# Second block: bias tables from one window per head, kept masks, norms beside the next values, residuals a tile ahead and slabs issued by ScalarE

## The chip, the cores and the metric

One of the eight cores of a Trainium2 chip runs the whole program. Its engines are TensorE (PE: matrix products and transposes into PSUM), VectorE (DVE), ScalarE (ACT), GpSimd (POOL) and SyncE (SP), which issues DMA transfers. Each engine works through its own list of instructions in order and waits on semaphores. The metric is device microseconds (us) of one execution; the profiler's span goes from the first to the last instruction of one profiled execution.

## The reference, cut to what matters

Two blocks run one after the other on a sequence of 1024 tokens, 1024 wide. The first block (dilated attention and a state-space mixer) is not touched. The second block has two layers; the first also carries a context of 256 tokens to a new value, the second does not.

```python
def hybrid_layer(x, xc, c_act, cc_act, w_mod, b_mod, w_in, conv_w, conv_b,
                 ret_decay, na_rpb, w_out, ln_g, ln_b, need_ctx):
    shift, scale, gate = jnp.split(c_act @ w_mod + b_mod, 3, axis=-1)
    h = x * (1 + scale[:, None]) + shift[:, None]
    rk, rv, nk, nv, rq, rg, nq, ng, ch, cb, ccg, cz = split_cols(h @ w_in, PROJ_SPLITS)
    ...
    y_conv = short_conv_branch(ch, cb, ccg, cz, conv_w, conv_b)
    y_ret, yc_ret = retention_branch(...)       # 6 heads, both directions, chunks of 128,
                                                # head_norm(o) * silu(g)
    y_na, yc_na = neighbourhood_branch(...)     # 6 heads, window of 8 x 16 on a 16 x 64 grid, plus the context
    y = jnp.concatenate([y_conv, y_ret, y_na], axis=-1) @ w_out
    x_new = layer_norm(DEEPNORM_ALPHA * x + gate[:, None] * y, ln_g, ln_b)
```

In the neighbourhood branch the score of a query and a key is their product times 1/8, plus a learned bias `rpb[head, dr, dc]` that depends on the difference of rows and columns alone; keys outside the window are left out, and one softmax goes over the 128 keys of the window and the 256 of the context.

## The kernel before, in words

`hybrid()` runs once for each layer. Every product with a weight is done as three products of rounded parts: `w_split` (L154, L155) has ACT round a raw weight tile `wr` to `wh` and DVE take the rest `wl`; the activations lie in SBUF as `aTh` and `aTl` (context: `cTh`, `cTl`). `project` runs 24 matmuls of 128x512 (L168) for each half of the tokens and 24 of 128x256 for the context, into the PSUM tag `mm` of two buffers.

Stages of a layer: the first half of the convolution; three pairs of retention heads (`ret_pair`); three pairs of neighbourhood heads (`na_project`, `na_core`), the second half of the convolution beside the last; `out_ln`, the output projection, residual and layer norm. The branches write their outputs, already gated, to `yd` in DRAM.

Work beside the projections stands in a list `bg` of small functions. While the matmuls of a projection are written, `tick` takes the next function from the list every eight matmuls, at the rate that `pace` sets; `drain` runs what is left. A scheduler then orders the instructions of each engine, so that the written order is a guide and not the order itself.

Retention: `raw` copies a projected group (ACT, tile `raw`), and `values`, `keys` and `queries` work on groups of 4, 4 and 2 chunks of 128 tokens. `queries` has five steps: f1 turns the group (transposes `T` on PE, L1515) and rotates it to `rq` with DVE and POOL; f2 turns it back (`qT`, `qw`); f3 makes the scores `S` (L1640) and `PD`; f4 makes the outputs from `PD` and the running states `St` (L1604, L1655, L1658), copies them (`oe`, ACT L1661), transposes them (`O` on PE, L1664) and makes the head norm: square (`sqr`, ACT), sum (`hv`, DVE), rstd (`hv`, POOL L1672, L1673), scaled output `cen` (DVE L1675); f5 transposes `cen` (L1684), multiplies by the gate `sgl` and stores to `yd`. The list `turns` sets in which order the steps of the three groups are taken; the last one is (2, 4), or (1, 4) in the layer without a context output, and `drain` ends a pair before the next pair's values.

Neighbourhood attention: a unit is one of 2 x 4 blocks of 128 queries (`rt`, `m`) for two heads. `s1` makes the scores against the context and the local keys (`S`, L1786) and DVE joins scores and table (`nsb`, L1766, with a running minimum `nmn`); ACT takes the exponent (`nsb`, L1769); `s2` transposes the weights (`T`, L1799, L1800; copies `nPT`, `nPX`), `s3` multiplies with the values `nV`. `nV` is made by `vturn` (L1730), the keys and queries `nk`, `nkz`, `nqq` by `split` (L1480).

A table `tab` holds bias and mask for 128 queries x 3 column places x 384 keys. `tables(rt)` (L1743 to L1753) is called for rt = 0 ahead of a pair's units and for rt = 1 at its third step. It loads the mask (one buffer) and, for each of the two heads, three slices of the padded bias by overlapping rows, and has DVE make 8 x bias + mask in place. All these loads are issued by SP, in its list among weight, gate and output transfers.

`out_ln`: `fetch` (L1947, L1948) loads slabs of `yd` for 256 tokens, `put` (L1951, L1952) rounds them into `aTh` and `aTl`, and the old activations' place is used again. Then for each tile of 128 tokens: load x into a slab's room (L2001, SP), 2 x 24 matmuls, gate product `ys` (DVE L2007), x and sum (L2008), mean (POOL L2014), square (ACT L2016), the norm with the next layer's scale and shift (L2019, L2020), the transposes into `aT` for the next layer (`to_aT`, L215 to L221), and the layer's own output (L2022, L2024), stored to x (L2025). The norm of a tile is written one tile later, as `pend`.

## Time and profile before

| | us |
|---|---|
| median of 3 runs (lowest, highest) | 3215.74 (3212.7, 3221.98) |
| the profiled execution's own time | 3217.48 |
| its span | 3215.5 |
| PE busy in the span | 3103.7 |
| mean granted PE clock | 0.988 of full speed |
| second block | about 1745 to 3215.5 |
| layer 0: retention, neighbourhood, projection | 1831 to 2095, to 2402, to 2550 |
| layer 1: retention, neighbourhood, projection | 2601 to 2846, to 3118, to 3215.5 |

All times in rows are microseconds from the span's start unless marked ns. A row of the timeline gives start, duration, engine, line, operation, written and read tile, the number of like instructions, and in brackets how long the engine stood idle before it and what let it go. A row of the list of waits is a sum over all waits of that kind.

### The profile page before, as it was taken

The numbers are of one execution on the slowest core, as the hardware profiler recorded it, in microseconds if no ns is written. First come the engines' busy times: TensorE is split into PE (matmuls) and PEld (weight loads), VectorE is DVE, ScalarE is ACT, GpSimd is POOL, SyncE is SP. The second block draws the span as 40 slices with busy tenths as digits, with TensorE's granted clock in tenths as the row PEclk, the third lists the DMA queues.
The fourth block names the chain that finished last, engine by engine and source line by source line (L and its number), as shares of the span: only waits on it lengthen the run. The fifth ranks groups of instructions, "written<-read, shape, count | busy, mean of one in ns | idle before, by whom it ended". The sixth has DMA issues, their size and how long they took to land. (4 is left out here: it accounts for less than half of the span.)

```text
span 3215.5 us, 47884 instructions
## 1 busy us (share of the span) xinstructions
PE 3103.7 (97%) x18100; PEld 2549.1 (79%) x18100; DVE 1898.8 (59%) x4099; ACT 1194.1 (37%) x2494; POOL 592.2 (18%) x769
## 2 busy tenths in 40 slices
PE   8999999999999999999999999999999999899998
PEld 6777878777877888787878888878877888778777
DVE  4676686677666658555544544454557854445455
ACT  4222555554555545322432122244352212134351
POOL 0364121112111101111002033300002212210001
PEclk9999999999999999999999999999999999999999
DMA  5465233233233235564442211142234321132232
GB/s 198 149 198 169 65 97 88 80 107 96 80 97 97 74 120 172 178 177 132 150 131 82 69 47 56 42 121 78 62 106 144 101 68 53 47 106 84 76 110 99
DMA packets 338907, 338.02 MB, mean 105 GB/s; under 512 B 29209, under 2 KB 278772, under 8 KB 338676
## 3 DMA queue, kind: packets, MB, share of 16 engines
q1 hardware_dynamic: 338676, 334.97, 34.1%
q8 instruction: 142, 2.33, 0.3%
q14 instruction: 89, 0.73, 0.1%
HBM read 262.22 MB, written 72.67 MB: 104 GB/s over the span
## 5 line engine op out<-in xcount | busy, mean ns | idle before, releaser
L168 PE MATMUL mm<-aTh,wh 128*128 128x512 f32 x2304 | 920.7, 400 | 18.2 <-DVE nk L1480 2.8
L168 PE MATMUL mm<-aTl,wh 128*128 128x512 f32 x2304 | 917.4, 398 | 0.4 <-DVE aTl L221 0.2
L168 PE MATMUL mm<-aTh,wl 128*128 128x512 f32 x2304 | 916.1, 398 | 0.7 <-DVE wl L155 0.7
L168 PEld LDWEIGHTS mm<-aTh,wh 128*128 128x128 f32 x2304 | 437.5, 190 | 110.2 <-issue 5.4
L168 PEld LDWEIGHTS mm<-aTh,wl 128*128 128x128 f32 x2304 | 436.8, 190 | 88.5 <-issue 3.4
L168 PEld LDWEIGHTS mm<-aTl,wh 128*128 128x128 f32 x2304 | 437.7, 190 | 85.3 <-issue 2.9
L155 DVE TENSOR_TENSOR wl<-wr,wh 128x1024 fp32r<-128x1024 f32 x158 | 196.8, 1245 | 191.4 <-ACT wh L154 190.8
L154 ACT ACTIVATE wh<-wr 128x1024 fp32r<-128x1024 f32 x158 | 166.9, 1057 | 329.6 <-PE mm L168 268.3
L475 ACT ACTIVATE sb<-sb,st 128x128 f32<-128x128 f32 (+1 forms) x384 | 170.1, 444 | 259.1 <-DVE st L473 257.3
L168 PE MATMUL mm<-wo,aTh 128*128 128x512 f32 x768 | 241.8, 396 | 7.1 <-DVE ys L2007 3.8
L1205 DVE SCALAR_TENSOR_TENSOR ma<-mw,cact,ma 128x256 f32<-128x256 f32 x336 | 182.4, 547 | 18.1 <-DMA mw<-in_w_mod 12.0
L168 PEld LDWEIGHTS mm<-wo,aTh 128*128 128x128 f32 x768 | 143.9, 190 | 38.1 <-DVE ys L2007 3.9
L473 DVE CUSTOM_DVE_ANT_0 sb<-S,bt 128x128 f32<-128x128 f32 (+1 forms) x384 | 125.2, 345 | 46.3 <-PE T L486 30.2
L168 PE MATMUL mm<-wo,aTl 128*128 128x512 f32 x384 | 151.4, 394 | 0.9 <-DVE aTl L1952 0.9
L427 POOL CAST qk<-kz 64x512 fp32r<-64x512 f32 x64 | 64.6, 1009 | 360.3 <-ACT kz L421 342.6
L1769 ACT ACTIVATE nsb<-nsb,nmn 128x640 f32<-128x640 f32 (+1 forms) x108 | 85.6, 793 | 118.8 <-DVE nmn L1766 106.3
L486 PE MATMUL T<-ident,sb 128*128 128x128 f32 x560 | 104.6, 283 | 12.0 <-DVE mr L1216 4.5
L168 PE MATMUL mm<-vh,aTl 128*128 128x512 f32 x288 | 114.5, 398 | 0.0
L168 PE MATMUL mm<-vh,aTh 128*128 128x512 f32 x288 | 113.8, 395 | 0.0
L168 PE MATMUL mm<-vl,aTh 128*128 128x512 f32 x288 | 113.6, 394 | 0.0
L168 PE MATMUL mm<-cTh,wl 128*128 128x256 f32 x352 | 101.7, 289 | 0.6 <-DVE wl L155 0.6
L168 PE MATMUL mm<-cTl,wh 128*128 128x256 f32 x352 | 101.9, 289 | 0.0
(448 smaller groups left out, 5701.4 us busy)
## 6 DMA issues: line engine op xcount, KB each, us to landing
wr<-in_attn_w_in SPq DMA_DIRECT2D x80, 512.0 KB
wr<-in_w_in SPq DMA_DIRECT2D x64, 512.0 KB
mw<-in_w_mod SPq DMA_DIRECT2D x48, 512.0 KB
tab<-in_c_rpb SPq DMA_DIRECT2D x72, 192.0 KB
vd<-vo SPq DMA_DIRECT2D x48, 256.0 KB
Wb<-wgd SPq DMA_DIRECT2D x96, 128.0 KB
x<-x SPq DMA_DIRECT2D x24, 512.0 KB
x<-in_x SPq DMA_DIRECT2D x16, 512.0 KB
```

The costliest lines, as they stand in the source:

```text
L154: nc.scalar.activation(h, raw, AF.Copy)
L155: nc.vector.tensor_tensor(l, raw, h.bitcast(F32), op=ALU.subtract)
L168: nc.tensor.matmul(out, s_, m_, start=first and i == 0, stop=last and i == len(todo) - 1)
L427: nc.gpsimd.tensor_copy(at(t[o], g, hf), at(h_[r], g, hf))
L473: nc.vector.tensor_tensor_reduce(out=sb[:, :N], in0=sp[:, a * 256:a * 256 + N], in1=b, scale=1.0, scalar=3e38, op0=ALU.add, op1=ALU.min, a ...
L475: nc.scalar.activation(sb[:, :N], sb[:, :N], AF.Exp, bias=mc, scale=-1.0, accum_out=st[:, 1, g, a, n:n + 1])
L486: nc.tensor.transpose(t[:, c:c + 128], Ps[a][:, b * 128:b * 128 + 128], self.ident)
L1205: V.scalar_tensor_tensor(a, L[h][:, k], c, a, op0=ALU.mult, op1=ALU.add)
L1769: ACT.activation(sb[:, :n], sb[:, :n], AF.Exp, bias=mc, scale=-1.0, accum_out=den)
```

## The change

The diff touches `na_masks`, `ret_pair`, `tables`, the calls around them, `fetch` and `out_ln`; the first block is as before.

- Tables: the order of the three column places is turned round, so that the three slices of a head's bias lie in one window of 400 columns (`win`, one load of 128x400) and are read from there by an overlapping view. The two masks of a layer are loaded once, in two buffers. `tables` no longer loads for itself: `fetch(p, rt)` is called right after the previous table is made, one table ahead; `tab` has one buffer for each head instead of two. The second table of a pair is made at the units' fifth step, not the third, and the first one after the values' turns.
- Norms: the last step f5 of a pair's last group is put into `tail` and run four places into the next pair's values, with three empty steps ahead of it. `turns` takes the steps in a slightly changed order.
- The tiles `raw`, `rr`, `k`, `rq` lie in a pool of their own (`early`).
- `out_ln`: x of the next tile is asked for one tile ahead, of the first before the loop; both gate products of a tile are written ahead of its two residual sums.
- Slabs: `fetch` of `yd` is issued by ACT, not SP.

```diff
-        for y, m in enumerate((0, 1, 3)):
+        for y, m in enumerate((3, 1, 0)):
...
+                early = rs.enter_context(tc.tile_pool(name=self.uid("re"), bufs=1, reuse_waits="tile"))
...
+                    if tail:
+                        self.bg.extend([idle, idle, idle, tail.pop()])
+                        self.rate = 1.0
                     raw(values, True)
...
-                    turns = ((0, 0), (0, 1), (1, 0), (0, 2), (0, 3), (1, 1), (2, 0), (0, 4), (1, 2), (1, 3), (2, 1),
-                             (1, 4), (2, 2), (2, 3), (2, 4))
-                    self.bg.extend(late[g][k] for g, k in turns if g < len(late))
+                    turns = ((0, 0), (0, 1), (0, 2), (1, 0), (0, 3), (1, 1), (2, 0), (1, 2), (0, 4), (1, 3), (2, 1),
+                             (2, 2), (1, 4), (2, 3), (2, 4))
+                    turns = [t for t in turns if t[0] < len(late)]
+                    self.bg.extend(late[g][k] for g, k in turns[:-1])
+                    tail.append(late[-1][4])
...
-                self.pace(9 if need_ctx else 6)
+                self.bg.extend([idle, idle, idle, tail.pop()])
+                self.pace(11 if need_ctx else 8)
...
+                masks = [wp.tile([128, 3, 384], F32, name=self.uid("mask"), tag=f"mask{rt}") for rt in range(2)]
+
+                def fetch(p, rt):
+                    TB[p, rt] = []
+                    for a in range(2):
+                        t = wp.tile([128, 400], F32, tag=f"win{a}", name=self.uid("win"))
+                        dr = (0 if rt == 0 else 4) - 8 * rt + 7
+                        off = rpb.offset + (l * 6 + 2 * p + a) * 896 + (6 + dr) * 32 - 1 - 239
+                        src = bass.AP(tensor=rpb.tensor, offset=off, ap=[[32, 8], [1, 16], [1, 400]])
+                        nc.sync.dma_start(t, src)
+                        TB[p, rt].append(t)
+                for rt in range(2):
+                    nc.sync.dma_start(masks[rt], A["c_namask"][:, rt * 3:rt * 3 + 3])
+                    if not rt:
+                        fetch(0, 0)
...
                     def tables(rt):
-                        def f():
-                            mask = wp.tile([128, 3, 384], F32, name=self.uid("mask"), tag="mask")
-                            nc.sync.dma_start(mask, A["c_namask"][:, rt * 3:rt * 3 + 3])
-                            for a in range(2):
-                                t = wp.tile([128, 3, 384], F32, tag=f"tab{a}", name=self.uid("tab"), bufs=2)
-                                for y in range(3):
...
-                                    nc.sync.dma_start(t[:, y], src)
-                                V.scalar_tensor_tensor(t, t, 8.0, mask, op0=ALU.mult, op1=ALU.add)
+                        for a, t in enumerate(TB.pop((p, rt))):
+                            o = wp.tile([128, 3, 384], F32, tag=f"tab{a}", name=self.uid("tab"))
+                            win = bass.AP(tensor=t.tensor, offset=t.offset, ap=[list(t.ap[0]), [8, 3], [1, 384]])
+                            V.scalar_tensor_tensor(o, win, 8.0, masks[rt], op0=ALU.mult, op1=ALU.add)
+                            L["tab", rt, a] = o
+                        if rt == 0:
+                            fetch(p, 1)
+                        elif p < 2:
+                            fetch(p + 1, 0)
...
-                    out = [tables(0), vturn(0), vturn(1), cturn, vturn(2), vturn(3)]
+                    out = [vturn(0), vturn(1), cturn, vturn(2), vturn(3), lambda: tables(0)]
...
-                            if i == 2:
-                                tables(1)()
+                            if i == 4:
+                                tables(1)
...
             def fetch(y, t):
-                nc.sync.dma_start(y[:, 0], yv[:, 0, t:t + 256])
-                nc.sync.dma_start(y[:, 2:8], yv[:, 2:8, t:t + 256])
+                ACT.dma_start(y[:, 0], yv[:, 0, t:t + 256])
+                ACT.dma_start(y[:, 2:8], yv[:, 2:8, t:t + 256])
...
+        xh = fetch()
         for ctx, i in tiles:
...
-            nc.sync.dma_start(x, src[i * 128:(i + 1) * 128, :])
+            if n < len(tiles):
+                xh = fetch()
...
                 V.tensor_tensor(hs[:, c], ps, B["gate"][:, c], op=ALU.mult)
+            for nh in range(2):
+                c = slice(nh * 512, nh * 512 + 512)
                 V.scalar_tensor_tensor(hs[:, c], x[:, c], alpha, hs[:, c], op0=ALU.mult, op1=ALU.add,
```

The order of the instructions moves with it. PE at the end of layer 1's second retention pair, before (`O`, `oe`, `cen` are the norm of the pair's last group, `raw` the next pair's values, `mm` the next values' products):

```order
L1658 MATMUL S_24766<-qw_4328_24723,St_24517 64x128
L1684 MATMUL T_24729<-ident,cen_24700 128x128 x4
L1658 MATMUL S_24766<-qw_4329_24726,St_24518 64x128
L1664 MATMUL O_24785<-ident,oe_24783 128x128 x4
L1684 MATMUL T_24800<-ident,cen_24796 128x128 x4
L1515 MATMUL T_24852<-ident,raw_24841 128x128 x4
L1515 MATMUL T_24888<-ident,raw_24877 128x128 x4
L168 MATMUL mm_25103<-aTh,wh_24915 128x512
L168 MATMUL mm_25103<-aTl,wh_24915 128x512
L168 MATMUL mm_25103<-aTh,wl_24916 128x512
```

After, the same place, up to the first products (the line numbers are those of the changed kernel, six higher here):

```order
L1664 MATMUL S_24753<-qw_4338_24710,St_24504 64x128
L1664 MATMUL S_24753<-qw_4339_24713,St_24505 64x128
L1521 MATMUL T_24832<-ident,raw_24821 128x128 x4
L1670 MATMUL O_24772<-ident,oe_24770 128x128 x4
L168 MATMUL mm_25090<-aTh,wh_24902 128x512
L168 MATMUL mm_25090<-aTl,wh_24902 128x512
```

and 24 products later:

```order
L168 MATMUL mm_25090<-aTl,wh_24902 128x512
L168 MATMUL mm_25090<-aTh,wl_24903 128x512
L1690 MATMUL T_24841<-ident,cen_24783 128x128 x4
L1521 MATMUL T_24875<-ident,raw_24864 128x128 x4
L1521 MATMUL T_24917<-ident,raw_24900 128x128 x2
```

The two transposes of the norm, next to each other before, have 24 matmuls between them, and one turn of `raw` stands ahead of the first.

DVE in the first units of layer 0's first neighbourhood pair, before (`nsb` joins scores and table, `nV` is a copy of values, `nqq` a query part):

```order
L1766 ISA nmn_19483 128x1
L1738 COPY nVc_19365<-T_19433 128x256
L1730 COPY nV_19364<-T_19445 128x512
L1762 ISA nsb_19510,nmn_19511<-S_19499,zero_16238 128x256
L1762 ISA nmn_19511 128x1
L1753 SCALAR_TENSOR_TENSOR tab_19549<-tab_19549,mask_19547 128x1152
L1753 SCALAR_TENSOR_TENSOR tab_19554<-tab_19554,mask_19547 128x1152
L1730 COPY nV_19364<-T_19451 128x512
L1766 ISA nsb_19510,nmn_19511<-S_19500,tab_19383,nmn_19511 128x384
```

After:

```order
L1793 ISA nmn_19491 128x1
L1771 COPY nVc_19377<-T_19421 128x256
L1763 COPY nV_19376<-T_19437 128x512
L1789 ISA nsb_19518,nmn_19519<-S_19507,zero_16238 128x256
L1789 ISA nmn_19519 128x1
L1763 COPY nV_19376<-T_19451 128x512
L1793 ISA nsb_19518,nmn_19519<-S_19508,tab_19457,nmn_19519 128x384
```

The second pair of table operations no longer stands between the softmax's rows and the second `nV`; the next ones come some twenty rows later.

DVE at the start of layer 0's projection, before, from tile 0's residual sums (`ys_22224` is tile 0, `ys_22281` tile 1, `ys_22190` the last slab):

```order
L2008 SCALAR_TENSOR_TENSOR ys_22224,ls_22226<-ys_22224 128x512 x2
L1952 TENSOR_TENSOR aTl<-ys_22190,aTh 128x6x256
L2019 SCALAR_TENSOR_TENSOR ys_22224<-ys_22224,ls_22226,nsc_22213 128x1024
L2007 TENSOR_TENSOR ys_22281<-mm_22284,gate_22211 128x512
L2007 TENSOR_TENSOR ys_22281<-mm_22311,gate_22211 128x512
L2020 SCALAR_TENSOR_TENSOR ys_22224<-ys_22224,rs_22343,nsh_22215 128x1024
L2022 SCALAR_TENSOR_TENSOR ys_22224<-ys_22224,ls_22226,ch_22207 128x1024
```

After, from the same instruction (`ys_22195` is tile 0, `ys_22210` tile 1, `ys_22174` the last slab):

```order
L2044 SCALAR_TENSOR_TENSOR ys_22195,ls_22212<-ys_22195 128x512 x2
L1979 TENSOR_TENSOR aTl<-ys_22174,aTh 128x256
L2055 SCALAR_TENSOR_TENSOR ys_22195<-ys_22195,ls_22212,nsc_22199 128x1024
L2058 SCALAR_TENSOR_TENSOR ys_22195<-ys_22195,ls_22212,ch_22191 128x1024
L2056 SCALAR_TENSOR_TENSOR ys_22195<-ys_22195,rs_22329,nsh_22201 128x1024
L1979 TENSOR_TENSOR aTl<-ys_22174,aTh 128x6x256
L2060 SCALAR_TENSOR_TENSOR ys_22195<-ys_22195,rs_22329,lb_22193 128x512 x2
L221 TENSOR_TENSOR aTl<-T_22333,aTh 128x4x128
L2041 TENSOR_TENSOR ys_22210<-mm_22270,gate_22197 128x512
L2041 TENSOR_TENSOR ys_22210<-mm_22296,gate_22197 128x512
```

Tile 1's gate products stood behind one step of tile 0's norm, and now stand behind all of it and a turned half for the next layer.

SP at the same place, before:

```order
L148 DMA wr_23098<-in_w_in 128x8x128
L1947 DMA ys_22197<-yd_16221 128x256
L1948 DMA ys_22197<-yd_16221 128x6x256
L148 DMA wr_23100<-in_w_in 128x8x128
L1947 DMA ys_22190<-yd_16221 128x256
L1948 DMA ys_22190<-yd_16221 128x6x256
L2001 DMA ys_22224<-x_11763 128x1024
L2001 DMA ys_22366<-x_11763 128x1024
```

After:

```order
L148 DMA wr_23078<-in_w_in 128x8x128
L148 DMA wr_23080<-in_w_in 128x8x128
L148 DMA wr_23082<-in_w_in 128x8x128
L148 DMA wr_23084<-in_w_in 128x8x128
L2014 DMA ys_22195<-x_11763 128x1024
L2014 DMA ys_22267<-x_11763 128x1024
```

The slabs (`ys` from `yd`) are no longer between the weights and x. On ACT, 18 slab issues stand where it had none: in layer 0 slab 1's two ahead of three weight roundings, slab 2's two behind them, those of slabs 3 and 4 ahead of the context's rounding.

## Rows read from the trace of the kernel before

**Rows 1.** The page: busy time; windows: sum over the second block.

```profile
PE 3103.7 (97%) x18100; PEld 2549.1 (79%) x18100; DVE 1898.8 (59%) x4099; ACT 1194.1 (37%) x2494; POOL 592.2 (18%) x769
...
sum 1470.50, PE 1419.06 PEld 1172.62 DVE 783.24 ACT 442.26 POOL 239.84; mean PE 177.38 PEld 146.58 DVE 97.91 ACT 55.28 POOL 29.98
```

**Rows 2.** Waits of PE, second block: us in total, times, longest.

```profile
PE T L1684 <- DVE cen L1675: 9.6, 3, 4.1
PE T L1799 <- DVE nPT L1803: 4.7, 1, 4.7
PE T L1800 <- DVE nV L1730: 4.0, 1, 4.0
PE mm L168 <- DVE ys L2007: 3.8, 2, 3.5
PE mm L168 <- DVE nk L1480: 2.8, 1, 2.8
PE mm L168 <- ACT nv L1455: 2.0, 1, 2.0
PE T L1515 <- POOL rq L1546: 1.6, 1, 1.6
PE mm L168 <- DVE nqq L1480: 1.6, 1, 1.6
PE T L1799 <- DVE nV L1730: 1.4, 1, 1.4
...
PE O L135 <- ACT nPT L1805: 1.4, 1, 1.4
PE O L1664 <- ACT oe L1661: 1.3, 2, 0.7
PE S L1640 <- DVE St L1604: 1.2, 1, 1.2
```

**Rows 3.** Windows: length, busy time (count) of five engines, PEclk, DMA share, GB/s.

```profile
2006.00:2014.00 8.00, 4.93 (x20) 3.81 (x21) 4.85 (x8) 1.54 (x4) 1.42 (x4) 0.79 0.48 137
2123.00:2139.00 16.00, 12.02 (x68) 9.85 (x67) 9.27 (x20) 8.08 (x14) 0.00 (x0) 0.79 0.41 117
```

**Rows 4.** The chain (start, us); timeline of a norm (start, us, engine, line, operation).

```profile
2568.79 32.48 PE mm L168 x142
...
2755.09 1.63 POOL L1673 TENSOR_TENSOR hv<-hv,mhalf 128x8 f32<-128x8 f32 x1
2757.50 1.11 PE L1684 MATMUL T<-ident,cen 128*128 128x128 f32 x4 [4.13 <-DVE cen L1675]
```

**Rows 5.** Timeline of DVE at two pairs of tables.

```profile
2123.84 2.63 DVE L1753 SCALAR_TENSOR_TENSOR tab<-tab,mask 128x1152 f32<-128x1152 f32 x2 [7.51 <-DMA mask<-in_c_namask]
...
2872.54 2.63 DVE L1753 SCALAR_TENSOR_TENSOR tab<-tab,mask 128x1152 f32<-128x1152 f32 x2 [5.84 <-issue]
```

**Rows 6.** Timeline of DVE and PE at the start of layer 0's projection.

```profile
2429.03 0.69 DVE L2008 SCALAR_TENSOR_TENSOR ys<-ys 128x512 f32<-128x512 f32 x1 [1.98 <-DMA ys<-x]
...
2430.26 1.75 DVE L1952 TENSOR_TENSOR aTl<-ys,aTh 128x1536 fp32r<-128x1536 f32 x1
2432.18 1.28 DVE L2019 SCALAR_TENSOR_TENSOR ys<-ys,ls,nsc 128x1024 f32<-128x1024 f32 x1 [0.17 <-POOL ls L2014]
2433.38 1.28 DVE L2007 TENSOR_TENSOR ys<-mm,gate 128x512 f32<-128x512 f32 x2
2434.57 1.28 DVE L2020 SCALAR_TENSOR_TENSOR ys<-ys,rs,nsh 128x1024 f32<-128x1024 f32 x1
...
2434.12 1.22 PE L168 MATMUL mm<-wo,aTh 128*128 128x512 f32 x2 [3.45 <-DVE ys L2007]
```

**Rows 7.** Timeline of SP at the same place: DMA issues, time in issue.

```profile
2405.73 9.21 SPq L148 DMA_DIRECT2D wr<-in_w_in  x3
...
2420.78 11.57 SPq L2001 DMA_DIRECT2D ys<-x  x3
```

**Rows 8.** Windows: the transfers at the same place, columns as in group 3.

```profile
2406.00:2414.00 8.00, 6.75 (x32) 5.03 (x31) 8.00 (x9) 5.12 (x6) 0.14 (x1) 1.00 1.02 370
```

26 lines of the change are left out of this document (14 added, 12 removed).

## The prediction

> **What bounds the kernel now.** I read the profile from the outside in. The table by engine has PE (TensorE) busy for 97% of the span and no other engine over 60% [rows 1], so the time ends where PE stands still. The diff touches only the second block, which runs from about 1745 us to the end; there PE is busy 1419.1 of 1470.5 us [rows 1], so 51.4 us are idle. That and the clock (below) are the ceiling for what can be won by taking waits away. Next comes the list of what PE waited for [rows 2]. It names a few single waits, not a steady loss: three for the centred outputs of retention (9.6 us in all), five that hang on DVE's (VectorE's) work in neighbourhood attention (nPT 4.7, nV 4.0 and 1.4, nk 2.8, nqq 1.6), one at the output projection (ys 3.5), and small ones. The last look is the granted clock: in the 8 us after the wait at 2006 it is 0.79 of the full 2.4 GHz, and the same over the 16 us after the wait at 2123 [rows 3]. Windows of 8 us at 2753, 2806 and 3017 and of 16 us at 2430 and 2870 read 0.79 too. So PE runs for a while at the lower level, 1.2 GHz, after each wait of 2.0 us or more but one (1926); after those of 1.4 to 1.6 us it does not. Lost are 0.21 x 8 = 1.7 us or 0.21 x 16 = 3.4 us. Some of that lies within the wait itself, where PE loses nothing, so I count three quarters: 1.3 and 2.5 us.
>
> **Norms beside the next values.** At a pair's end the last head group goes through O transposes on PE, then square, sum, rstd and centring on ACT, DVE, POOL and DVE, then T cen on PE. Before, O and T cen stand next to each other on PE, and T cen waits 4.13 us, 1.63 of them in one POOL row [rows 4]. The others are 2.84 us and 2.62 us (9.6 - 4.13 - 2.84). After, 24 value matmuls of 128x512 stand between them. A matmul takes 32.48/142 = 0.229 us [rows 4], so the cover is 5.5 us against a chain of 4.1. All three waits go: -9.6 us. The two waits of O for oe (1.3 us in all) each get four transposes of raw as cover, 0.44 us: -0.9. The move takes a cover away elsewhere: in layer 0's second pair the middle group's T cen now comes some 2.4 us after its O, so 4.1 - 2.4 = 1.7 us of new wait, short enough not to touch the clock. Clock: two windows, -2.5. What is late next is the raw copy on ACT behind T raw, well under 1 us. Sum **-11.3 us** (bounds -13 and -5).
>
> **Bias tables and masks.** Before, each unit pair loads a mask (576 KB) and six tables (192 KB each) through single buffers, so the mask's issue waits on SP for DVE's reading of the old table, and the table operation waits for the landing with DVE's whole queue behind it. The rows show it: DVE stands 7.51 us for a mask, then spends 2.63 us on two tables, and only then copies nV, for which PE waits 4.0 us; at 2872 the same gives nPT, 4.7 us [rows 5, 2]. For nk, nqq and the nV of 1.4 us it is the wait for a table's landing ahead of them on DVE. After, two masks stay for the layer, a head needs one window of 128x400 (200 KB), and it is asked for one table earlier: 12 mask loads become 4, 72 loads become 24. Queued bytes fall from 12 x 576 + 72 x 192 KB = 20.7 MB to 7.1 MB. On SP the window's issue still waits for the reading of its buffer, but that reading is just over when SP gets there; behind it stand weights and gate stores with many us to spare. The second table is built at unit 4 rather than 2, its DVE work no longer in front of nV. The 24 table operations keep their shape, at 1.3 us [rows 5]; the strided window could cost nothing or double that, on an engine busy half of the stage, and I take nothing. The five waits go: 4.7 + 4.0 + 2.8 + 1.6 + 1.4 = 14.5 us, and clock 2.5 + 2.5 + 1.3 = 6.3. Second waiters will come through: units that wait for no table still show one of 1.4 us (nPT from ACT) [rows 2]; I give 0.7 back at each of five places, 3.5. Sum **-17.3 us** (bounds -21 and 0).
>
> **Query turns and states.** The new order of turns and the moved last query change three rows: rq 1.6, St 1.2, nv 2.0 [rows 2], with 1.3 of clock. The transpose of rq in layer 0 gets about 1.1 us more cover: -1.6 with the small shift of its engines. Half of St and nv: -1.6. In layer 1's third pair the first group's cover falls from 6.8 to 4.2 us; its chain has no wait in the rows, so it is shorter than 6.8; the norm's chain of 4.1 is the nearest on the other side. The price lies between 0 and 2.6, and I take 1.5. Sum **-1.7 us** (bounds -6 and +3).
>
> **Residuals a tile ahead.** At layer 0's projection PE waits 3.45 us for tile 1's gate product, which stands on DVE behind tile 0's residual; x of tile 0 was issued at 2420.78 and used at 2429.03, 8.25 us later [rows 6, 7]. Now SP has four weight loads and then x, without the two slabs that took most of 2414.94 to 2420.78 [rows 7]. So x is issued 0 to 5.8 us earlier; I take 4.5, as one more weight remains in front: landing 2424.5. But the order of DVE changes against it. Before, tile 1's gates start 4.35 us after the residual (2433.38 - 2429.03). After, they stand behind tile 0's whole norm. From the landing: 3.15 to the first product (2432.18 - 2429.03), two products of 1.2 each with the slab's remainder between, 1.2 for the shift by rstd, 1.75 for that remainder, two of 0.69 for the last step, 0.69 for the copy of a transposed half, 0.69 for the gate: about 11.2 with the overlaps in the rows [rows 6]. The wait begins at 2434.12 - 3.45 = 2430.7. With 2424.5 the gate is there at 2435.7, a wait of 5.0 instead of 3.45: **+1.6 us**. The ends: x at 2419 or sooner, wait and clock gone, -6; x at 2429, a wait of 9.5, +6. Later tiles have DVE time to spare.
>
> **Slabs by ScalarE's queue.** 18 issues move to ACT. The trace before has no issue on ACT; SP's took (9.21 + 11.57)/6 = 3.46 us each where the transfers were densest [rows 7], and the other end is nothing. ACT is busy 442 of 1470 us [rows 1], and most of these issues stand where it would idle. Slab 1's pair stands ahead of three weight roundings and slab 2's behind them, so the conv rounding that PE needs comes later by an issue or two. Slab 1's are asked for while the queue is not yet full, so I take a value near the lower end: **+0.5 us** (bounds 0 and +3.5).
>
> **Sum.** -11.3 - 17.3 - 1.7 + 1.6 + 0.5 = -28.2 us against the profiled execution's 3217.5 us, so 3189.3. That execution lies 1.7 us above the median of the runs shown: **3188 us** for a median.
>
> **Rivals.** First, **x lands no earlier**: the transfer engines had no time to spare then (share 1.02, 370 GB/s) [rows 8], and the slabs still share them. x at 2429, wait 9.5: 3188 + 4.5 = 3192 us. For it speaks that all of it is one set of bytes, against it that x now stands ahead of the slabs in SP's order.
>
> Second, **x overtakes the slabs**. Two issuing engines have two lists; if they are served in turn, x passes most of 1.8 MB of slabs and no wait is left: 3188 - 5.0 - 2.5 = 3180 us. No row of before shows two lists at work. The Trainium skill ("DMA: Bandwidth & Descriptors", section "Queues, rings and completion order") says that each DMA engine goes round-robin between the queue rows it has work for, a packet at a time; by that rule this rival is what happens, and the sum would be about 3180. The same page ("Issuing engines are not separate DMA queues") says that starting DMAs from several engines saves only the issue time; by that, slab bytes land no sooner in all.
>
> Third, **the tables are still late**: the windows and masks land in memory that retention frees late, and SP holds the first ones until then. All of that part comes back: 3188 + 17.3 = 3205 us. Against it: the first tables are used at about 2108, some 15 us after the first issue.
>
> Fourth, **the norm's wait only moves**: with the value matmuls in front, the raw transposes or the next group's values end last, +11.3: 3199 us.
>
> Fifth, **ACT is held by its own loads**, on the slower side. At the two projections 14 slab issues stand ahead of roundings that PE needs. If each takes 3.46 us, as SP's did, and PE waits for it, 48.4 us: 3236 us. It ends slower from 2.7 us each on the path, (3225.4 - 3188)/14. Against it: SP's long issues came with its list full of slabs, weights and x at once.
>
> **Chances.** My forecast 0.52, x no earlier 0.16, x overtaking 0.10, tables late 0.12, norms 0.06, ACT held 0.04. A measurement can tell 0.3%, 9.6 us: faster is below 3206.1, slower above 3225.4. Tables late lies at that edge, so 0.05 of it counts as faster and 0.07 as the same: faster 0.89, same 0.07, slower 0.04. The range 3173 to 3205 takes in the bounds of projection and turns at both ends; it leaves out ACT held, half of tables late and the corner in which every bound is a gain.
>
> **What would show it.** Right: no wait of PE for cen over 2 us; no DVE idle before the table operation over 1 us; a clock of 1.00 where 0.79 stood, but at layer 0's projection. Wrong: PE waits there that name the conv rounding or a weight on ACT; idle DVE before the first tables; a wait for the gate under 2 us or over 8.

## The result, and the profile after

| kernel | median, us (runs; lowest to highest) | ratio to before, 95% interval |
|---|---|---|
| before | 3216.9 (4; 3212.7 to 3221.98) | |
| after | 3182.31 (4; 3176.36 to 3182.93) | 0.9889 [0.9876, 0.9901] |

The change makes the kernel 1.1% faster: 34.6 us by the medians, where 28 were forecast. It lies inside the range (3173 to 3205) and 5.7 us below the predicted 3188.

The span goes from 3215.5 to 3180.2 us, but a part of that difference is not the change's. Both kernels run the same instructions up to the second block, and yet its first product of the context's tokens (`mm<-cTh,wh`, L168) starts at 1749.1 us before and at 1752.7 after; in the profiled executions of all kernels below it lies between 1746.9 and 1755.7. So I compare second blocks, from that product to the end of the span. Window rows give them (length, then busy time and count of PE, PEld, DVE, ACT and POOL, granted clock, DMA share, GB/s). Before:

```profile
1749.10:3215.50 1466.40, 1414.96 (x8688) 1169.15 (x8686) 783.02 (x1583) 440.95 (x771) 238.40 (x298) 0.99 0.27 82
```

After:

```profile
1752.70:3180.20 1427.50, 1399.66 (x8689) 1160.58 (x8686) 787.04 (x1583) 439.46 (x769) 245.93 (x298) 0.99 0.24 74
```

The second block is 38.9 us shorter. PE stands still for 27.8 us of it instead of 51.4 (1427.50 - 1399.66 and 1466.40 - 1414.96): -23.6. And it is busy 15.3 us less for the same products. The forecast's -28.2 was made of -19.4 for waits and -8.8 for the clock. Against 38.9 it is 10.7 short; the median shows less of that, as the first block of the profiled execution ran 3.6 us longer. (In the second group of runs below, the median of the same kernel lies 38.7 us under that of before.) Below, "idle" and "busy" of a kernel are these two numbers.

The waits of PE in the second block of after (total, times, longest), against [rows 2]:

```profile
PE mm L168 <- DVE ys L2041: 4.9, 2, 2.5
PE T L215 <- DVE ys L2056: 3.1, 1, 3.1
PE mm L168 <- ACT nv L1455: 1.7, 1, 1.7
PE T L1521 <- POOL rq L1552: 1.5, 1, 1.5
...
PE mm L168 <- ACT raw L1514: 0.7, 1, 0.7
PE T L1690 <- DVE cen L1681: 0.6, 1, 0.6
...
PE O L1670 <- ACT oe L1667: 0.2, 1, 0.2
```

The norm's `cen` falls from 9.6 to 0.6 us and `oe` from 1.3 to 0.2. None of the five waits for tables is left: no `nPT`, `nV`, `nk` or `nqq` stands in the list. The largest that are left are at the output projections: the gate product `ys` (4.9 in two, one in each layer) and the turned rows of the norm (3.1).

The windows of [rows 3] in after, and the start of layer 0's projection:

```profile
2006.00:2014.00 8.00, 6.76 (x39) 5.39 (x34) 4.37 (x7) 1.56 (x4) 1.79 (x7) 1.00 0.35 100
2123.00:2139.00 16.00, 16.00 (x111) 12.40 (x109) 9.25 (x26) 9.03 (x19) 0.61 (x1) 1.00 0.20 55
...
2418.00:2434.00 16.00, 11.47 (x38) 9.12 (x39) 14.13 (x20) 2.63 (x5) 2.66 (x4) 0.68 0.35 111
```

Where 0.79 stood, 1.00 stands; at layer 0's projection the lower level is left, as the prediction had said of that place (0.68 as the mean of 16 us). The kernel after does not reach the same work at the same time, so I also went through its whole second block in windows of 4 us: the clock is under 0.9 only between 2420.7 and 2432.7 and in the last 7.5 us. PE's share of the span on the page is 97%, as in [rows 1], because the span shrank with its busy time.

```profile
PE 3089.3 (97%) x18100; PEld 2541.0 (80%) x18100; DVE 1906.7 (60%) x4099; ACT 1192.0 (37%) x2492; POOL 598.4 (19%) x769
```

### The profile page after: what moved, and what is told of

Same layout as the page of the kernel before. It is cut to its first block, busy times and chain, and to the rows that moved or that the text cites. A ratio compares the mean times of both kernels' runs of the same rounds, so it can differ in the third digit from the quotient of the medians.

```text
span 3180.2 us, 47784 instructions
## 1 busy us (share of the span) xinstructions
PE 3089.3 (97%) x18100; PEld 2541.0 (80%) x18100; DVE 1906.7 (60%) x4099; ACT 1192.0 (37%) x2492; POOL 598.4 (19%) x769
## 5 line engine op out<-in xcount | busy, mean ns | idle before, releaser
L168 PE MATMUL mm<-aTh,wh 128*128 128x512 f32 x2304 | 918.9, 399 | 12.4 <-ACT yr L639 3.6
L168 PE MATMUL mm<-aTl,wh 128*128 128x512 f32 x2304 | 915.8, 398 | 0.2 <-DVE aTl L1072 0.2
L168 PE MATMUL mm<-aTh,wl 128*128 128x512 f32 x2304 | 915.2, 397 | 0.6 <-DVE wl L155 0.6
L168 PEld LDWEIGHTS mm<-aTh,wh 128*128 128x128 f32 x2304 | 436.4, 189 | 104.8 <-issue 4.9
L168 PEld LDWEIGHTS mm<-aTh,wl 128*128 128x128 f32 x2304 | 435.9, 189 | 86.8 <-issue 2.4
L168 PEld LDWEIGHTS mm<-aTl,wh 128*128 128x128 f32 x2304 | 436.2, 189 | 84.7 <-issue 2.7
L168 PE MATMUL mm<-wo,aTh 128*128 128x512 f32 x768 | 243.5, 399 | 9.8 <-DVE ys L2041 4.9
L1205 DVE SCALAR_TENSOR_TENSOR ma<-mw,cact,ma 128x256 f32<-128x256 f32 x336 | 182.9, 548 | 19.4 <-DMA mw<-in_w_mod 13.3
L168 PEld LDWEIGHTS mm<-wo,aTh 128*128 128x128 f32 x768 | 144.5, 191 | 41.7 <-DVE hs L1154 4.5
L168 PE MATMUL mm<-wo,aTl 128*128 128x512 f32 x384 | 151.8, 395 | 0.5 <-DVE aTl L1979 0.4
L168 PE MATMUL mm<-vh,aTl 128*128 128x512 f32 x288 | 114.7, 398 | 0.0
L168 PE MATMUL mm<-vh,aTh 128*128 128x512 f32 x288 | 114.1, 396 | 0.0
L168 PE MATMUL mm<-vl,aTh 128*128 128x512 f32 x288 | 113.6, 395 | 0.0
L168 PE MATMUL mm<-cTh,wl 128*128 128x256 f32 x352 | 100.8, 286 | 0.6 <-DVE wl L155 0.6
L168 PE MATMUL mm<-cTh,wh 128*128 128x256 f32 x352 | 101.3, 288 | 0.0
```

The source lines that it names most:

```text
L168: nc.tensor.matmul(out, s_, m_, start=first and i == 0, stop=last and i == len(todo) - 1)
L1205: V.scalar_tensor_tensor(a, L[h][:, k], c, a, op0=ALU.mult, op1=ALU.add)
```

## The experiments

Twelve kernels ran in three groups; those of a group shared a chip and its runs of before. The second block's numbers are from the profiled execution of each.

| kernel | group: before | median, us | ratio, 95% interval | second block | busy | idle |
|---|---|---|---|---|---|---|
| before | | | | 1466.4 | 1415.0 | 51.4 |
| after | | 3182.31 | 0.9889 [0.9876, 0.9901] | 1427.5 | 1399.7 | 27.8 |
| tables_only | 1: 3220.94 | 3195.83 | 0.9916 [0.9902, 0.9929] | 1440.8 | 1406.6 | 34.2 |
| norms_only | 1 | 3200.78 | 0.9935 [0.9922, 0.9949] | 1449.5 | 1406.4 | 43.1 |
| projection_only | 1 | 3215.89 | 0.9984 [0.9974, 0.9993] | 1463.6 | 1414.0 | 49.6 |
| after_slabs_sp | 1 | 3175.87 | 0.9853 [0.984, 0.9867] | 1421.1 | 1396.9 | 24.2 |
| after_again | 2: 3220.01 | 3181.29 | 0.9879 [0.9864, 0.9893] | 1425.9 | 1398.1 | 27.8 |
| after_masks | 2 | 3181.26 | 0.9884 [0.9868, 0.9901] | 1428.0 | 1399.7 | 28.3 |
| after_second_table_early | 2 | 3181.61 | 0.9884 [0.9869, 0.9899] | 1428.8 | 1399.2 | 29.7 |
| gates_first | 2 | 3172.22 | 0.9851 [0.9836, 0.9866] | 1417.4 | 1395.6 | 21.8 |
| before_tables_late | 3: 3220.01 | 3195.69 | 0.992 [0.9906, 0.9935] | 1438.9 | 1401.4 | 37.5 |
| after_one_pool | 3 | 3180.03 | 0.9876 [0.986, 0.9891] | 1425.4 | 1397.9 | 27.5 |
| tables_and_norms | 3 | 3174.9 | 0.9857 [0.9841, 0.9873] | 1420.8 | 1397.0 | 23.8 |
| gates_first_act | 3 | 3173.39 | 0.9853 [0.9834, 0.9872] | 1423.1 | 1398.5 | 24.6 |

### One part at a time

**tables_only** is the kernel before with the tables' part alone (windows, kept masks, `tables` at the fifth step) and the pool `early`:

```diff
-                    out = [tables(0), vturn(0), vturn(1), cturn, vturn(2), vturn(3)]
+                    out = [vturn(0), vturn(1), cturn, vturn(2), vturn(3), lambda: tables(0)]
...
-                            if i == 2:
-                                tables(1)()
+                            if i == 4:
+                                tables(1)
```

> The kernel before with the table part alone (windows, kept masks, second table at unit 4, the pool for early tiles). My theory: the waits for nPT, nV, nk, nqq and the 1.4 us for nPT from ACT go (15.9 us) with three stretches at the lower clock (about 6.5 us), and nothing else moves: 22 us faster, a ratio near 0.993; no PE wait on DVE work of the neighbourhood stage over 1 us. Rival (the parts overlap, and some of that gain belongs to the moved norms and turns): 8 to 14 us faster.

Measured: the second block is 25.6 us shorter, idle -17.2, busy -8.4. Over both neighbourhood stages (2095 to 2410 and 2850 to 3100) PE's list of waits holds one row, which is the projection's:

```profile
PE mm L168 <- ACT aTh L1972: 1.0, 1, 1.0
```

So all five waits went, and nothing came in their place. By the medians the kernel is 25.1 us under its before.

**norms_only** is the kernel before with the moved last step, the new order of turns and `early`:

```diff
+                    if tail:
+                        self.bg.extend([idle, idle, idle, tail.pop()])
+                        self.rate = 1.0
                     raw(values, True)
...
-                    self.bg.extend(late[g][k] for g, k in turns if g < len(late))
+                    self.bg.extend(late[g][k] for g, k in turns[:-1])
+                    tail.append(late[-1][4])
```

> The kernel before with the norm part alone (last step beside the next values, new turns, the pool for early tiles). My theory: waits for cen fall from 9.6 to about 0.6 us, those for oe from 1.3 to 0.2, and the two stretches at the lower clock behind them go: 12 to 15 us faster, a ratio near 0.996. Rival (the wait only moves to the raw copies and to query steps): under 6 us faster.

Measured: the second block is 16.9 us shorter, idle -8.3, busy -8.6. PE's waits, the three largest and the norm's:

```profile
PE mm L168 <- ACT nv L1455: 8.2, 2, 6.5
PE T L1812 <- DVE nV L1742: 5.0, 1, 5.0
PE mm L168 <- DVE nk L1480: 4.5, 3, 3.8
...
PE T L1690 <- DVE cen L1681: 0.6, 1, 0.6
```

`cen` is as small as in after. But the neighbourhood stages came out differently, with 6.5, 5.0 and 4.5 us in these three rows alone where [rows 2] has 14.5 in five; I take shifted loads for the cause, and did not test it. The total of this profile is therefore not the price of the norms alone. A better reading is tables_and_norms (below) against tables_only: 1440.8 - 1420.8 = 20.0 us, idle -10.4 and busy -9.6. The medians say the same: norms_only is 20.2 us under its before (12 to 15 were expected), tables_only 25.1, and tables_and_norms 45.1, so these two parts add.

**projection_only** is the kernel before with slabs on ACT, x a tile ahead and both gate products ahead of both sums:

```diff
-                nc.sync.dma_start(y[:, 0], yv[:, 0, t:t + 256])
-                nc.sync.dma_start(y[:, 2:8], yv[:, 2:8, t:t + 256])
+                ACT.dma_start(y[:, 0], yv[:, 0, t:t + 256])
+                ACT.dma_start(y[:, 2:8], yv[:, 2:8, t:t + 256])
...
-            nc.sync.dma_start(x, src[i * 128:(i + 1) * 128, :])
+            if n < len(tiles):
+                xh = fetch()
```

> The kernel before with the residual part and the slabs by ScalarE, and nothing else. My theory: at layer 0's projection x lands some 2 us earlier against TensorE, but tile 1's gates now stand behind tile 0's norm, so the wait of 3.45 becomes about 5.5 us; at layer 1 a new wait of about 2.5 us for the first gate behind a late slab: 3 to 6 us slower, a ratio near 1.0015. Rival (x overtakes the slabs, the wait goes): 5 to 8 us faster.

This one missed: the second block came out 2.8 us shorter, not longer (about 5 us by the medians). The forecast wait for a gate at layer 1's projection isn't in its trace either. PE's two rows at layer 0's projection (start, length, operation, idle before):

```profile
2433.39 1.06 PE L215 MATMUL T<-ident,ys 128*128 128x128 f32 x8 [3.16 <-DVE ys L2029]
2437.58 1.19 PE L168 MATMUL mm<-wo,aTh 128*128 128x512 f32 x2 [3.13 <-DVE ys L2014]
```

The projection's own wait did grow as forecast, from 3.45 to 6.3 us [rows 6]. What outweighed it lies in the neighbourhood stages: the wait for `nk` (2.8 us) is gone, that for `nV` is down from 4.0 to 1.5, and in place of the 4.7 for `nPT` stands one of 4.1:

```profile
PE S L1786 <- DVE nmn L1762: 4.1, 1, 4.1
...
PE T L1800 <- DVE nV L1730: 1.5, 1, 1.5
```

These waits go with the tables' part anyway, so the projection's part alone can't be added to the others: -25.6 - 16.9 - 2.8 = -45.3 us against -38.9 for all.

### Tables: the loads, or the place of the operation?

The prediction put the tables' waits down to late landings: many bytes, single buffers, an issue that waits. A second reading is that the operation stood too early in DVE's list. **before_tables_late** tells them apart: it keeps the kernel before with all its loads, bytes and buffers, and only places the table operations, behind the last softmax row written before them, and the second table at the fifth step:

```diff
-                                V.scalar_tensor_tensor(t, t, 8.0, mask, op0=ALU.mult, op1=ALU.add)
+                                with self.tc.issue_after(last["soft"].ins) if last else ExitStack():
+                                    V.scalar_tensor_tensor(t, t, 8.0, mask, op0=ALU.mult, op1=ALU.add)
...
-                            V.tensor_tensor_reduce(out=sb[:, 256:640], in0=Lc, in1=tab, scale=-0.125, scalar=mc,
+                            last["soft"] = V.tensor_tensor_reduce(out=sb[:, 256:640], in0=Lc, in1=tab, scale=-0.125, scalar=mc,
...
-                            if i == 2:
+                            if i == 4:
                                 tables(1)()
```

> The kernel before with one thing changed: the two table operations of each table but the first are held on VectorE until the last softmax row that read the table before. All loads, buffers and bytes are those of before. Theory of place (an operation that waits for its load stood too far ahead in VectorE's list, with nV and nPT behind it): the waits of 4.0 and 4.7 us, and 1.4 to 2.8 us of the others, go with the lower clock behind them, 14 to 20 us faster than the kernel before, ratio 0.994 to 0.996. Theory of loads (the transfers were too large or too late, as my prediction had it): the operations still wait for masks or tables, now later, under 6 us faster.

Measured: 27.5 us off the second block, as much as the tables' part with its new loads (25.6). The profiled execution is the fastest of its six; by the medians it is 24.3 us against 25.1. The view of the tile `tab` sums how long DVE stood idle ahead of the operations that read or write it, and until what. Before:

```profile
  DMA tab<-in_c_rpb: 53.2, 16
...
  DMA mask<-in_c_namask: 7.5, 1
  issue: 5.8, 1
```

before_tables_late:

```profile
  DMA tab<-in_c_rpb: 9.0, 4
```

After (the operation reads `win` there):

```profile
  DMA win<-in_c_rpb: 5.0, 2
```

Of 66.5 us of idle DVE, 57.5 go without a byte less being loaded. DVE's list in the first units shows how (compare [rows 5]):

```profile
2116.82 0.41 DVE L1764 CUSTOM_DVE_ANT_0 nsb<-S,zero 128x256 f32<-128x256 f32 x1
...
2120.58 0.69 DVE L1731 COPY nV<-T 128x512 f32<-128x512 f32 x1 [3.35 <-PE T L1730]
```

Where before two table operations stood and waited 7.51 us for their mask, DVE now waits for PE and copies `nV` at once. The five waits of [rows 2] are down to one of 1.5 us (`nqq`) and one of 1.1 (`nV`).

**after_masks** puts the twelve mask loads back into after, into the same two buffers:

```diff
+                    masks[rt] = wp.tile([128, 3, 384], F32, name=self.uid("mask"), tag=f"mask{rt}")
+                    nc.sync.dma_start(masks[rt], A["c_namask"][:, rt * 3:rt * 3 + 3])
                     TB[p, rt] = []
```

> The changed kernel with a mask of 576 KB loaded again for every table, one table ahead like the windows: 12 mask loads instead of 4. My theory (what counts is that the load is asked for one table ahead, into memory that is free): no wait for a table over 1 us comes back, 0 to 2 us slower than the changed kernel. Rival (what counts is the number of bytes): waits for the mask of 2 us and more come back at several of the 12 tables, 6 to 15 us slower.

No difference (1428.0 against 1427.5 and 1425.9 of two profiles of after). The eight loads of 576 KB that the change saves are worth nothing that these runs can tell.

**after_second_table_early** moves the second table of after back to the third step:

```diff
-                            if i == 4:
+                            if i == 2:
                                 tables(1)
```

> The changed kernel with the second table of a pair made at the third step of the units again, as before. My theory (the loads were the cause): the two table operations stand ahead of nV on VectorE but find their data, 2.6 us of work; PE waits 0 to 1 us at each of six places, 0 to 4 us slower than the changed kernel. Rival (the place was the cause): the waits of 4.0 and 4.7 us come back with the lower clock behind them, 12 to 15 us slower.

It decided nothing: the instructions of PE, DVE and ACT came out in the same order as in after. `tab` has one buffer for each head there, so the new table can't be made ahead of the last row that reads the old one, wherever its call is written. Its 1428.8 us are a third sample of after. So no run here has the small, early loads with the operation at its old place.

That points at what in the change did the work. With two buffers, and the load landing in the table itself, the operation could be placed well ahead of its first reader; one buffer pins it behind the last reader of the table before. (Argued from the orders; one buffer alone was not run.) **after_one_pool** takes the pool `early` away, to see whether the memory that retention frees sooner had a share:

```diff
-                            t = early.tile([128, 512], F32, tag="raw", name=self.uid("raw"), bufs=4)
+                            t = rp.tile([128, 512], F32, tag="raw", name=self.uid("raw"), bufs=4)
```

(and the same for `rr`, `k` and `rq`).

> The changed kernel with the tiles raw, rr, k and rq back in the pool of the other retention tiles; the order of instructions is the same. My theory (the first masks and windows wait for the memory under them): the first tables of a layer find their data late, a wait of VectorE of up to 5 us at two places and of TensorE of 1 to 4 us there, 2 to 6 us slower than the changed kernel. Rival (there is slack between retention's end and the first table): no change within 1 us.

1425.4 us: no share. I had given it 2 to 6 us, and that was wrong.

### The projection: slabs on ACT, residuals ahead

**after_again** is after once more, on the second group's chip.

> The changed kernel as it is, for the comparison with the others on one chip. Every theory: 34 to 39 us faster than the kernel before, ratio 0.988 to 0.990, and the waits of its first trace again (3.1 and 2.4 us at layer 0's projection, 2.5 us at layer 1's).

1425.9 us and 3181.29 in the median: this is what to compare in that group. The waits at layer 0 came again (3.33 and 2.60 us); that at layer 1 is 1.30 us, not 2.5. In the five profiles of kernels with after's order on PE and DVE it lies between 1.30 and 2.89.

**after_slabs_sp** is after with the slabs back on SP:

```diff
-                ACT.dma_start(y[:, 0], yv[:, 0, t:t + 256])
-                ACT.dma_start(y[:, 2:8], yv[:, 2:8, t:t + 256])
+                nc.sync.dma_start(y[:, 0], yv[:, 0, t:t + 256])
+                nc.sync.dma_start(y[:, 2:8], yv[:, 2:8, t:t + 256])
```

> The changed kernel with the slabs issued by SP again. The scheduler then puts tile 1's gates of layer 0 ahead of most of tile 0's norm, as before the change. My theory (moving the slabs to ScalarE cost time): the wait at layer 0 falls from 5.5 to about 3.5 us and that of 2.5 us at layer 1 goes: 3 to 6 us faster than the changed kernel, about 39 us faster than the kernel before, ratio near 0.988. Rival (a second queue brings the slabs or x sooner): 3 to 8 us slower than the changed kernel, ratio near 0.991.

It is faster than after: 4.8 to 6.4 us in the second block. Moving the slabs costs time, in two places. At layer 0 the scheduler orders DVE differently when ACT issues the slabs. DVE of after (start, length, line, operation, idle before):

```profile
2413.76 0.69 DVE L2044 SCALAR_TENSOR_TENSOR ys<-ys 128x512 f32<-128x512 f32 x1 [1.49 <-DMA ys<-x]
...
2418.72 1.28 DVE L2056 SCALAR_TENSOR_TENSOR ys<-ys,rs,nsh 128x1024 f32<-128x1024 f32 x1 [0.46 <-POOL rs L196]
...
2422.92 0.68 DVE L221 TENSOR_TENSOR aTl<-T,aTh 128x512 fp32r<-128x512 f32 x1
2423.52 1.27 DVE L2041 TENSOR_TENSOR ys<-mm,gate 128x512 f32<-128x512 f32 x2
```

PE of after:

```profile
2420.15 1.82 PE L215 MATMUL T<-ident,ys 128*128 128x128 f32 x8 [3.11 <-DVE ys L2056]
2424.34 1.19 PE L168 MATMUL mm<-wo,aTh 128*128 128x512 f32 x2 [2.37 <-DVE ys L2041]
```

DVE of after_slabs_sp:

```profile
2415.45 0.69 DVE L2044 SCALAR_TENSOR_TENSOR ys<-ys 128x512 f32<-128x512 f32 x1 [1.92 <-DMA ys<-x]
...
2418.60 1.28 DVE L2055 SCALAR_TENSOR_TENSOR ys<-ys,ls,nsc 128x1024 f32<-128x1024 f32 x1 [0.17 <-POOL ls L2050]
2419.80 1.28 DVE L2041 TENSOR_TENSOR ys<-mm,gate 128x512 f32<-128x512 f32 x2
```

With the slabs on SP tile 1's gates (L2041) follow one step of tile 0's norm, 4.35 us after x's landing, the same distance as before the change [rows 6]; with the slabs on ACT they follow all of it, 9.76 us after. PE waits 3.78 us in the one and 3.11 + 2.37 = 5.48 in the other (4.8 to 6.8 in the five profiles with that order).

At layer 1 a wait is new. ACT of after, with its issues (ACTq):

```profile
3078.77 1.06 ACT L1978 ACTIVATE aTh<-co 128x1024 fp32r<-128x1024 f32 x1
3079.71 0.35 ACTq L1974 DMA_DIRECT2D ys<-yd  x1
...
3080.11 0.47 ACTq L1975 DMA_DIRECT2D ys<-yd  x1
...
3089.44 1.49 ACT L1978 ACTIVATE aTh<-ys 128x1536 fp32r<-128x1536 f32 x1 [3.44 <-DMA ys<-yd]
```

and PE:

```profile
3093.38 0.73 PE L168 MATMUL mm<-wo,aTh 128*128 128x512 f32 x2 [2.51 <-DVE ys L2041]
```

An issue itself is cheap (0.35 and 0.47 us). But it stands in ACT's list behind roundings of weights and values, and the slab is asked for when these are done. SP of after_slabs_sp asks for the same piece at:

```profile
3071.12 0.43 SPq L1975 DMA_DIRECT2D ys<-yd  x1
```

Rows of after lie 4.3 us later at that place (the first rounding of a slab there: 3065.20 against 3060.94), so this is 3080.11 - 3071.12 - 4.3 = 4.7 us sooner. In after the piece lands at 3089.44, DVE rounds its rest, the gate product stands behind that on DVE, and PE waits 2.51 us. In after_slabs_sp the gate product stands behind the same rest, but that is done by 3083.42 (the row holds both pieces of the slab), and the gate waits for PE:

```profile
3081.33 2.09 DVE L1979 TENSOR_TENSOR aTl<-ys,aTh 128x256 fp32r<-128x256 f32 x2
...
3085.24 0.69 DVE L2041 TENSOR_TENSOR ys<-mm,gate 128x512 f32<-128x512 f32 x1 [1.83 <-PE mm L168]
```

So DVE's order is the same at this place, and the wait comes from the late issue.

**tables_and_norms** takes the rest of the projection's part back as well: slabs on SP, and x and the sums as before.

```diff
-            if n < len(tiles):
-                xh = fetch()
+            nc.sync.dma_start(x, src[i * 128:(i + 1) * 128, :])
...
-            for nh in range(2):
-                c = slice(nh * 512, nh * 512 + 512)
                 V.scalar_tensor_tensor(hs[:, c], x[:, c], alpha, hs[:, c], op0=ALU.mult, op1=ALU.add,
```

> The changed kernel without its projection part (slabs by SP, x asked for at its own tile, gate and residual sum in turn). My theory (slabs by ScalarE cost time, x a tile ahead is worth little): 3 to 5 us faster than the changed kernel, 41 to 44 us faster than the kernel before. Rival (the projection part pays on the whole): 1 to 4 us slower than the changed kernel.

1420.8 us, and a wait of 3.7 at layer 0: the same as after_slabs_sp. So asking for x a tile ahead, with the slabs on SP, is worth nothing. Nor does it ask sooner: in both traces SP issues the last slab's larger piece right ahead of x (2407.11 and 2407.63 in after_slabs_sp, 2406.13 and 2406.65 here). On this chip all four runs of tables_and_norms (3172.38 to 3176.61) lie below all four of after_one_pool (3179.49 to 3183.05), which has after's order: **the projection's part costs about 5 us**, and the moved slabs are its cause.

**gates_first** has the slabs on SP and x a tile ahead, and puts tile 0's residual sums behind tile 1's gate products:

```diff
-                V.tensor_tensor(hs[:, c], ps, B["gate"][:, c], op=ALU.mult)
+                gated = V.tensor_tensor(hs[:, c], ps, B["gate"][:, c], op=ALU.mult)
...
+            if first:
+                with self.tc.issue_after(gated.ins):
+                    first.pop()()
+            if nxt and n == 1:
+                first.append(residual)
+            else:
+                residual()
```

> The changed kernel with the slabs issued by SP and, at layer 0's projection, tile 0's residual sums queued on VectorE behind tile 1's gate products. My theory (the wait there is the order on VectorE behind x's landing): the wait of 3.8 us that stays with the slabs on SP falls under 1.5 us and the stretch at the lower clock goes: 3 to 5 us faster than that kernel, 9 to 12 us faster than the changed kernel. Rival (the late slab ahead of the gates holds them as well, or the next step ends as late): 0 to 1 us faster than with the slabs on SP alone.

DVE, with the sums now behind the gates, and the window of the place:

```profile
2412.08 1.29 DVE L2041 TENSOR_TENSOR ys<-mm,gate 128x512 f32<-128x512 f32 x2
```

```profile
2418.00:2434.00 16.00, 16.00 (x76) 13.18 (x75) 14.70 (x21) 3.57 (x6) 5.83 (x8) 1.00 0.32 100
```

PE's wait is 1.07 us, and the clock stays at 1.00. The second block is 1417.4 us. All four runs (3166.77 to 3174.65) lie below all four of after_again (3176.82 to 3182.19) on the same chip, by 9.1 us in the median: this version beats both kernels.

**gates_first_act** makes the same edit and leaves the slabs on ACT.

```diff
-                V.tensor_tensor(hs[:, c], ps, B["gate"][:, c], op=ALU.mult)
+                gated = V.tensor_tensor(hs[:, c], ps, B["gate"][:, c], op=ALU.mult)
...
+                with self.tc.issue_after(gated.ins):
+                    first.pop()()
```

> The changed kernel, slabs by ScalarE as it has them, with tile 0's residual sums at layer 0's projection queued behind tile 1's gate products. My theory: of the two waits there (3.1 and 2.4 us) at most 1.5 us stays and the lower clock behind them goes, 5 to 7 us faster than the changed kernel; layer 1's wait of 2.5 us behind the late slab stays. So it is 3 to 4 us slower than the same order with the slabs on SP. Rival (the second queue alone makes x late): under 2 us faster than the changed kernel.

Layer 0's wait goes here too, so that wait was the order's and not the queue's. Layer 1's stays:

```profile
3081.68 1.22 PE L168 MATMUL mm<-wo,aTh 128*128 128x512 f32 x2 [2.98 <-DVE ys L2041]
```

The second block is 1423.1 us, 5.7 more than gates_first in the profiles. The medians, 3173.39 and 3172.22 on different chips, don't tell the two apart, so the price of layer 1's late issue rests on the profiles alone. On its own chip all four runs of gates_first_act (3170.51 to 3175.79) lie below all four of after_one_pool, by 6.6 us in the median.

## Why the prediction was right, and where it was not

**What bounds the kernel** held: PE's standstill and its clock in the second block. The gain is -23.6 us idle and -15.3 busy, most of the latter the clock (last section).

**Norms** (forecast -11.3 with the clock). The waits went as reckoned: `cen` -9.0, `oe` -1.1; the raw copy that was to be late next is 0.7 us. Of the forecast new wait of 1.7 us nothing over 0.6 is to be seen. Beside the tables' part, norms and turns together bring -20.0 us (13.0 forecast): idle -10.4 where the waits of both came to -10.5 (-8.8 and -1.7), and busy -9.6 where the clock was given -2.5. **The mis-sized term is the clock**, not the wait. The forecast took two windows of 8 us. In tables_only four places of the retention stages are at the lower level: the three whose rows stand in the last section, and 0.79 over the 8 us from 2014. They lose 0.21 x (8 + 16 + 16 + 8) = 10.1 us. In tables_and_norms both retention stages read 1.00:

```profile
1751.73:2090.00 338.27, 332.97 (x2199) 279.79 (x2198) 167.89 (x347) 71.58 (x124) 87.09 (x112) 1.00 0.19 57
2590.00:2830.00 240.00, 237.97 (x1601) 199.11 (x1600) 111.42 (x239) 53.33 (x89) 68.90 (x72) 1.00 0.19 56
```

The last section shows why this term can't be read from one trace.

**Tables** (forecast -17.3). The five waits went, 14.5 us, and with them one of 1.4 that I had left standing. The 3.5 us of second waiters never came: PE's list of tables_only has none in these stages. Alone, the part brings -25.6 us. So the size was short by a third: idle -17.2 against -11.0, busy -8.4 against -6.3. **The cause was put in the wrong place.** The prediction argued from queued bytes (20.7 to 7.1 MB), buffers and early issues, and named the later place of the second table only in passing. before_tables_late gains as much with all the old loads, so the place is enough; after_masks loses nothing with the masks loaded again, so their bytes don't count. Whether the new loads would have been enough at the old place isn't shown. The step that failed is to ask why the load was late, and not why the list came to it so early: in [rows 5] DVE waits 7.51 us for a mask, and the copy of `nV` behind it, which needs no table, could have run.

**Query turns and states** (forecast -1.7). `St` (1.2), layer 0's `rq` (1.6) and layer 1's `nv` (2.0) are gone. New are an `rq` of 1.5 in layer 1's third pair, as taken, and an `nv` of 1.7 in layer 0 where `rq` had stood, which was not. That makes -1.6 us, and the agreement is luck: half of `St` and `nv` had been left standing, and layer 0's new wait was not foreseen. The 1.3 us of clock that the prediction names there are not in its sum. The order of turns alone leaves the instruction order of every engine as it was (seen in the program, not in a run), and so does the pool for PE (after_one_pool); what acts is the moved last step.

**Residuals a tile ahead** (forecast +1.6). The wait was put at 5.0 us and is 5.48 in two pieces (4.8 to 6.8 in five profiles). x was to land 4.5 us earlier against the start of PE's wait. Before it landed 1.6 us ahead of that (2429.03 against 2430.67, [rows 6]); after, 3.3 ahead (2413.76 against 2420.15 - 3.11 = 2417.04): 1.6 us earlier. The chain from there to PE's next product took 10.6 us instead of about 11.2. So x was 2.9 us less early than taken (4.5 against 1.6) and the chain 0.6 shorter; and within the wait PE ran the eight transposes of tile 0's rows for 1.82 us (2420.15), which the forecast had not set against it: 5.0 + 2.9 - 0.6 - 1.8 = 5.5. That the wait came out near is luck. And I had put the new order of DVE down to this edit; after_slabs_sp shows that it comes from the slabs, and without their move the edit does not even ask for x sooner.

**Slabs by ACT's queue** (forecast +0.5, bounds 0 and 3.5). It cost 4.8 to 6.4 us, above the upper bound. The bound was made of the time that an issue takes. What cost was the place of the issue in ACT's list (4.7 us later in layer 1) and a different order on DVE (layer 0).

**Rivals.** x no earlier: no. x overtaking the slabs gave 3180 us, close to the 3182 measured, but its mechanism isn't there: x was issued at 2400.98, between four slab issues on ACT (2398.87 to 2403.43), and used at 2413.76:

```profile
2400.98 21.04 SPq L2014 DMA_DIRECT2D ys<-x  x3
```

That is 12.8 us from issue to use, against 8.25 before [rows 6, 7], and the wait for the gate did not vanish. The Trainium skill ("DMA: Bandwidth & Descriptors", section "Issuing engines are not separate DMA queues") says that transfers started by different engines interleave on the same DMA engines and that spreading them saves only issue time; this trace doesn't contradict it, with 12.8 us against 8.25, but four weight loads (2392.47 to 2400.89) stand ahead of x in SP's list, so it is no test of the rule alone. The round-robin that the Trainium skill states (same page, section "Queues, rings and completion order") may be at work as well, but it brought x no wait-free landing. The norm's wait only moved, and ACT held by its loads at 3.46 us each: neither is in the trace (ACT's two issues above take 0.35 and 0.47 us). Tables late is there once, at layer 1's first tables, where the prediction had asked for no idle DVE over 1 us:

```profile
2836.57 1.36 DVE L1777 SCALAR_TENSOR_TENSOR tab<-win,mask 128x1152 f32<-128x1152 f32 x1 [4.13 <-DMA win<-in_c_rpb]
```

With 0.86 us at the next table these are the 5.0 us in the view of `win`. No wait of PE follows between 2828 and 2870, so it cost nothing.

Added up: tables 8.3 us short, norms and turns 7.0 short, and the projection, forecast at +2.1, 6.7 us dearer than tables_and_norms, so 4.6 too cheap. That is 10.7 of 38.9 us, and errors of both signs made it smaller than its parts.

## What to carry to other kernels

When an engine stands idle for a transfer, first look at what stands behind the waiting instruction in its list and whether that was ready: moving the instruction to where its result is needed was worth as much here as the change that also made its load smaller and earlier. (That a second buffer is what lets a scheduler move it too far ahead is argued here, not shown.) A transfer issued by a computing engine is asked for only when that engine's list comes to it, so price the place in the list and not the issue. And where several parts remove waits, run them alone and together, since a part that only shifts transfers can borrow another part's gain.
